# S5 power tables summed in one piece and written by ScalarE; the x2 sums on VectorE

## The chip, the cores and the metric

The kernel runs on one core of a Trainium2 chip. The metric is device time in microseconds (us), the median of several executions. One more execution was taken with the hardware profiler; all rows below are of that one.

Engine names as in the profile: PE is TensorE (matmuls), PEld its weight loads, DVE is VectorE, ACT is ScalarE, POOL is GpSimd, SP is SyncE, which here only issues DMAs.

## The reference, cut to what matters

One transformer block on a sequence of 1024 rows of width 1024, in fp32: four mixers side by side (dilated attention, retention, gated linear attention, an S5 state space layer), an output projection and a norm; a cross attention to a memory of 256 rows and a norm; a SwiGLU feed-forward layer (inner width 2816) and a norm.

The two places that the change touches are the S5 layer and the way into the feed-forward layer.

```python
bu_re = jnp.einsum('bsgi,gpi->bsgp', ug, bb_re)
bu_im = jnp.einsum('bsgi,gpi->bsgp', ug, bb_im)
...
_, _, x_re, x_im = lax.associative_scan(combine, (at_re, at_im, bu_re, bu_im), axis=1)
y = (jnp.einsum('bsgp,gip->bsgi', x_re, c_re) - jnp.einsum('bsgp,gip->bsgi', x_im, c_im)
     + d * ug)
...
return (jax.nn.silu(x @ w_gate) * (x @ w_up)) @ w_down
```

S5 has 16 groups with 64 complex states and 16 channels each. The kernel takes the sequence in steps of eight, so it needs the powers 1 to 8 of each state's complex decay, times the input matrix (tables W) and times the output matrix (tables C).

## The kernel before, in words

**Order of the work.** The program is written as one Python class. `weave` interleaves, on PE, the steps of a mixer with matmul groups of the input projections (`fill_v`, `fill_fm`), so that PE has work while a mixer's small steps run on the other engines. The order in which each engine issues its instructions is then made by a planner with its own costs and simulated times; on the chip each engine works through its queue strictly in that order. fp32 matmuls are done as three products: `split` makes a rounded part on ScalarE (`whi`, `xv`: line 149) and the rest on VectorE (`wlo`, `xv`: line 150) from each operand.

**Buffers.** Tiles of 128 x 1024 come from one pool of 37 buffers through `big` (line 136), which begins each with a tiny GpSimd memset; these memsets are chained in program order, so a buffer that comes free late holds up all later ones. PSUM tiles of one tag have two buffers. Weights are loaded through three `wraw` buffers by SP's queue.

**S5 tables.** `s5_start` calls `s5_powers` four times: W for both halves h of the groups (products on VectorE), then C for both halves (products on GpSimd). Each call makes two tables (i = 0 and 1), each 128 partitions x 1024 columns. Partitions 0 to 63 hold one group of a pair (g = 0) and 64 to 127 the other (g = 1); the table has 32 columns for each power and each pair, 16 for g = 0 and 16 for g = 1, and where partition and column belong to different groups it is zero. Lines 1464 and 1465 form two products of 128 x 512 in a scratch tile `pab`; line 1468 zeroes with GpSimd the two quarters that must be zero, 64 x 512 each; lines 1473 to 1477 add or subtract the products with VectorE straight into the other two quarters, 64 x 512 each. That is two memsets and two sums for each of eight tables, 16 and 16 in all.

`s5_tables` (per half) transposes W on PE (`sV`), copies the result to SBUF with `copy`, which takes ScalarE and VectorE in turn (lines 185 and 186, two copies of 128 x 512 for each of four tables), multiplies W by a constant table on PE (`sK`), copies that (`sKt`, line 1502) on VectorE, and transposes it (`sKp`). `s5_rot` makes sines and cosines on VectorE and ScalarE. `s5_delays` loads shifted copies of the input (`s5D`) by DMA from `sur` in DRAM.

While this goes on, PE runs the projection `dv`: groups of 24 matmuls, its weights in three pieces. The third piece is 128 x 544, and its VectorE rest (`wlo`) is a VectorE instruction in the midst of the S5 tables.

**The turn to gate/up.** The feed-forward layer uses Strassen-like sums of blocks. `x2_turn` transposes the layer's input into four blocks `xr` (two tiles of 128 x 1024 each); `x2_sums` makes in place the differences T1 (`b12 - b11`), T2 (`b22 - T1`), T3 (`b22 - b12`) and T4 (`b21 - T2`), all by line 529, T1 and T2 on VectorE and T3 and T4 on GpSimd, and `x2_version` splits each into its two parts `xv` (ScalarE, then VectorE). `gu_first` runs for the first three of the column pairs while this goes on: matmuls with B11 into `gc`, copied to `ge` by ScalarE (line 681), then with B21 on top of it, then `h` (lines 686, 688). `gu_rest` uses the T products. GpSimd also makes sums of weight blocks (`sub`, line 631).

Of the kernel before, what the change touches and what calls it, by code (L numbers as in the profile page):

```python
# [15 lines left out]
ALU = mybir.AluOpType  # L16
PSUM = bass.MemoryType.PSUM

P = 128
# [18 lines left out]
class Kernel:  # L38
# [488 lines left out]

    def x2_sums(self):
        tt = lambda e, o, a, b, op: [e.tensor_tensor(out=o[i], in0=a[i], in1=b[i], op=op) for i in range(2)]
        v, g = self.nc.vector, self.nc.gpsimd  # L530
        b11, b12, b21, b22 = [self.xr[q] for q in ((0, 0), (0, 1), (1, 0), (1, 1))]
        tt(v, b11, b12, b11, ALU.subtract)
        self.x2_version("T1", b11)
        tt(v, b11, b22, b11, ALU.subtract)
        self.x2_version("T2", b11)
        self.qu = [self.big(n) for n in ("gq", "gu2")]
        tt(g, b12, b22, b12, ALU.subtract)
        self.x2_version("B22", b22)
        tt(g, b21, b21, b11, ALU.subtract)
        self.x2_version("T3", b12)  # L540
        self.x2_version("T4", b21)
        self.xr = None
# [911 lines left out]
    def s5_powers(self, src, t0, j0, neg, s, eng):  # L1454
        nc, v = self.nc, self.nc.vector
        pr, pi = [self.s5[q][:, j0:j0 + 4, t0:t0 + 8].unsqueeze(3).to_broadcast([P, 4, 8, 16]) for q in ("pr", "pi")]
        xr, xi = [src[i][:, j0:j0 + 4, :].unsqueeze(2).to_broadcast([P, 4, 8, 16]) for i in range(2)]
        out = []
        for i in range(2):
            w = s[i]  # L1460
            ab = self.big("pab")
            a, b = ab[:, :512], ab[:, 512:]
            a4, b4 = [q.rearrange("p (j t i) -> p j t i", j=4, t=8) for q in (a, b)]
            eng.tensor_tensor(out=a4, in0=pr, in1=(xr, xi)[i], op=ALU.mult)
            eng.tensor_tensor(out=b4, in0=pi, in1=(xi, xr)[i], op=ALU.mult)
            w4 = w.rearrange("p (j t i) -> p j t i", j=4, t=8)
            for g in range(2):
                nc.gpsimd.memset(w4[64 * g:64 * g + 64, :, :, 16 - 16 * g:32 - 16 * g], 0.0)
            for g in range(2):
                r = slice(64 * g, 64 * g + 64)  # L1470
                o = w4[r, :, :, 16 * g:16 * g + 16]
                if i == 0:
                    v.tensor_tensor(out=o, in0=a4[r], in1=b4[r], op=ALU.subtract)
                elif neg:
                    v.scalar_tensor_tensor(out=o, in0=a4[r], scalar=-1.0, in1=b4[r], op0=ALU.mult, op1=ALU.subtract)
                else:
                    v.tensor_tensor(out=o, in0=a4[r], in1=b4[r], op=ALU.add)
            out.append(w)
        return out

    def s5_tables(self, h):
        v = self.nc.vector
        j0 = 4 * h
        W, Cp = self.s5w[h]
        Vw = []
        kt = self.tr("sK").rearrange("p a b -> p (a b)")[:, :256]
        for i in range(2):
            o = self.big("s5V")
            t = self.two("sV")
            for b in range(2):  # L1490
                for q in range(4):
                    c = (4 * b + q) * P
                    self.tp(t[:, c:c + P], W[i][:, c:c + P])
            for b in range(2):
                self.copy(o[:, b * 512:(b + 1) * 512], t[:, b * 512:(b + 1) * 512])
            Vw.append(o)
            for jj in range(4):
                self.mm(kt[32 * jj:32 * jj + 32], self.s5["c0"][i][:, j0 + jj, :], W[i][:, jj * 256:jj * 256 + 256],
                        start=i == 0, stop=i == 1, tile_position=(0, 32 * jj))
            yield 0.88  # L1500
        ks = self.half("sKt")
        v.tensor_copy(ks[:, :256], kt)
        yield 1.7
        kp = self.tr("sKp")
        for dd in range(2):
            self.tp(kp[:, dd, :], ks[:, dd * P:(dd + 1) * P])
        K = self.s5k[h]
        v.tensor_copy(K, kp[:, :2, :].rearrange("p a b -> p (a b)"))
        self.s5t.append((Vw, K.rearrange("p (b a c) -> p a b c", a=4, b=2), Cp))
# [110 lines left out]

    def s5_start(self):
        nc = self.nc
        W = [self.s5_powers(self.s5["bb"], 0, 4 * h, False, [self.big("s5W") for _ in range(2)], nc.vector)
             for h in range(2)]
        C = [self.s5_powers(self.s5["c"], 8, 4 * h, True, [self.big("s5C") for _ in range(2)], nc.gpsimd)
             for h in range(2)]
        self.s5w, self.s5t = list(zip(W, C)), []
        self.s5r = self.s5_rot(0)
        self.s5D = [self.big("s5D") for _ in range(4)]
        self.s5d3 = [d.rearrange("p (s c) -> p s c", c=P) for d in self.s5D]  # L1630
# [195 lines left out]
```

## Time and profile before

| what | value |
|---|---|
| time, median of 3 runs | 1474.85 us (1470.94 to 1479.25) |
| the profiled execution's own time | 1470.48 us |
| its span, first to last instruction | 1468.7 us |
| PE busy | 1428.1 us (97%) |
| DVE busy | 938.7 us (64%) |
| ACT busy | 522.0 us (36%) |
| POOL busy | 340.8 us (23%) |

The busy share of an engine is an average over stages that are limited by different things. What decides a stage is which engine the others wait for there. The time outside the span (1470.48 against 1468.7) is 1.8 us.

### The profile page before, as it was taken

To read this page: it belongs to the slowest core of one execution; us is meant where nothing else is said; L and a number is where in the kernel's file an instruction comes from. 1 tells how busy PE (TensorE), PEld (TensorE's weight loads), DVE (VectorE), ACT (ScalarE), POOL (GpSimd) and SP (SyncE) were. 2 spreads that over 40 slices of the span, in tenths; PEclk is the share of its full clock that TensorE was granted. 3 is DMA by queue.
4 is the path that set the end of the run, shared out by engine and by line. 5 is a ranking of instruction groups with operands and counts; after the bars stand their busy time and mean duration, and the time that the engine had idled before them with its cause. 6 is when DMAs were issued, how large, how long until landed. Compare 5 with 4: busy or idle time off the path is not lost.

```text
span 1468.7 us, 20723 instructions
## 1 busy us (share of the span) xinstructions
PE 1428.1 (97%) x7778; PEld 1167.7 (80%) x7778; DVE 938.7 (64%) x1622; ACT 522.0 (36%) x828; POOL 340.8 (23%) x598
## 2 busy tenths in 40 slices
PE   8699999999999999999999989999999999999997
PEld 6587778778788888888888768888888888888885
DVE  7978545475467479548557986576655556554557
ACT  4124433352244124334344532222222224434324
POOL 6300000010000000000000466776666640000003
PEclk9899999999999999999999999999999999999999
DMA  6442111010338302214312425544444447666612
GB/s 225 143 104 94 34 58 44 15 58 2 127 110 301 101 30 72 74 56 137 121 36 95 158 79 186 185 168 165 165 166 166 163 166 278 219 194 191 195 41 108
DMA packets 71508, 184.70 MB, mean 126 GB/s; under 512 B 8544, under 2 KB 9328, under 8 KB 71408
## 3 DMA queue, kind: packets, MB, share of 16 engines
q1 hardware_dynamic: 69680, 180.23, 37.1%
q10 hardware_dynamic: 1728, 3.15, 0.6%
q8 instruction: 61, 1.00, 0.3%
q14 instruction: 39, 0.32, 0.1%
HBM read 141.79 MB, written 41.55 MB: 125 GB/s over the span
## 4 chain that ended last, share of the span: by engine, by line
PE 85%; DVE 8%; DMA 3%; issue 2%; ACT 1%; POOL 1%; SPq 0%; DVEq 0%; POOLq 0%; ACTq 0%
PE ga L73 11%; PE fm L73 8%; PE gb L73 7%; PE gc L73 7%; PE da L73 7%; PE q L73 6%; PE wo L73 6%; PE mx L73 5%; PE dr L73 5%; PE dn L73 3%; PE ds L73 2%; PE gv L73 2%; PE s L73 2%; DVE wlo L150 2%; PE pv L73 1%
## 5 line engine op out<-in xcount | busy, mean ns | idle before, releaser
L150 DVE TENSOR_TENSOR wlo<-wraw,whi 128x1024 fp32r<-128x1024 f32 (+3 forms) x177 | 230.2, 1303 | 126.1 <-ACT whi L149 125.2
L149 ACT CAST whi<-wraw 128x1024 fp32r<-128x1024 f32 (+3 forms) x177 | 183.2, 1038 | 289.5 <-PE da L73 56.5
L73 PE MATMUL ga<-xv,whi 128*128 128x512 f32 x528 | 163.1, 390 | 3.8 <-DVE gq L696 3.8
L73 PEld LDWEIGHTS ga<-xv,whi 128*128 128x128 f32 x528 | 98.7, 188 | 26.1 <-issue 5.8
L73 PE MATMUL gc<-xv,whi 128*128 128x512 f32 x352 | 110.7, 396 | 5.1 <-ACT ge L681 5.0
L73 PE MATMUL gb<-xv,whi 128*128 128x512 f32 x352 | 108.4, 389 | 0.0
L73 PE MATMUL ga<-xv,wlo 128*128 128x512 f32 x264 | 102.8, 389 | 0.0
L73 PE MATMUL fm<-xh,whi 128*128 128x512 f32 x208 | 86.0, 414 | 0.0
L73 PEld LDWEIGHTS gc<-xv,whi 128*128 128x128 f32 x352 | 66.7, 191 | 20.0 <-ACT ge L681 6.0
L73 PE MATMUL wo<-whi,oT 128*128 128x512 f32 x256 | 82.1, 394 | 0.0
L73 PE MATMUL fm<-xh,wlo 128*128 128x512 f32 x208 | 81.5, 392 | 0.0
L73 PE MATMUL fm<-xl,whi 128*128 128x512 f32 x208 | 81.3, 391 | 0.0
L73 PE MATMUL mx<-whi,yT 128*128 128x512 f32 x256 | 80.6, 392 | 0.1
L73 PEld LDWEIGHTS gb<-xv,whi 128*128 128x128 f32 x352 | 66.1, 188 | 13.8
L73 PE MATMUL gc<-xv,wlo 128*128 128x512 f32 x176 | 69.2, 393 | 0.0
L73 PE MATMUL gb<-xv,wlo 128*128 128x512 f32 x176 | 68.5, 389 | 0.0
L263 POOL TENSOR_TENSOR X<-X,ln_ff_b 128x1024 f32<-128x1024 f32 x7 | 16.7, 2387 | 209.6 <-ACT X L262 209.6
L73 PEld LDWEIGHTS ga<-xv,wlo 128*128 128x128 f32 x264 | 49.6, 188 | 10.3
L73 PEld LDWEIGHTS mx<-whi,yT 128*128 128x128 f32 x256 | 48.1, 188 | 10.8 <-DVE V L150 0.5
L73 PE MATMUL da<-whi 128*128 128x512 f32 x144 | 56.2, 390 | 0.0
L73 PE MATMUL da<-whi,wlo 128*128 128x512 f32 x144 | 56.0, 389 | 0.0
L73 PE MATMUL da<-wlo,whi 128*128 128x512 f32 x144 | 56.0, 389 | 0.0
(500 smaller groups left out, 3332.3 us busy)
## 6 DMA issues: line engine op xcount, KB each, us to landing
wraw<-in_w_gu SPq DMA_DIRECT2D x28, 512.0 KB, 4.1
gr<-in_w_gu SPq DMA_DIRECT2D x22, 512.0 KB, 4.9
dw<-in_w_down SPq DMA_DIRECT2D x18, 512.0 KB, 3.7
tT<-dw SPq DMA_DIRECT2D x36, 256.0 KB, 2.0
wraw<-hS SPq DMA_DIRECT2D x36, 256.0 KB, 2.7
wraw<-tT SPq DMA_DIRECT2D x36, 256.0 KB, 3.0
wraw<-in_w_q SPq DMA_DIRECT2D x16, 512.0 KB, 4.3
wraw<-in_w_o SPq DMA_DIRECT2D x16, 512.0 KB, 3.5
```

What stands on the lines that cost most here:

```text
L73: return self.pin(self.nc.tensor.matmul(*a, **k))
L149: return (self.nc.scalar.copy(out=hi, in_=src), self.nc.vector.tensor_tensor(out=lo, in0=src, in1=hi.bitcast(F32), op=ALU.subtract))
L150: self.nc.vector.tensor_tensor(out=lo, in0=src, in1=hi.bitcast(F32), op=ALU.subtract))
L263: nc.gpsimd.tensor_tensor(out=x, in0=x, in1=b, op=ALU.add)
```

## The change

In `s5_powers` the two products are now added or subtracted once, over all 128 partitions, in place in `pab`. ScalarE then writes the sum twice, into the columns of g = 0 and of g = 1, each time multiplied by a column of a small table `gmul` with one value for each partition: 1 (or -1, for the negated tables) on the partitions of that group and 0 on the others. So the zeros come out of the multiplication, and the 16 memsets are gone. `gmul` (128 x 4) is made once by eight memsets of 64 x 1. In `s5_tables` all copies of `sV` are put on ScalarE. In `x2_sums` the sums of T3 and T4 move from GpSimd to VectorE.

```diff
     def x2_sums(self):
...
-        v, g = self.nc.vector, self.nc.gpsimd
+        v = self.nc.vector
...
-        tt(g, b12, b22, b12, ALU.subtract)
+        tt(v, b12, b22, b12, ALU.subtract)
         self.x2_version("B22", b22)
-        tt(g, b21, b21, b11, ALU.subtract)
+        tt(v, b21, b21, b11, ALU.subtract)
...
             eng.tensor_tensor(out=b4, in0=pi, in1=(xi, xr)[i], op=ALU.mult)
-            w4 = w.rearrange("p (j t i) -> p j t i", j=4, t=8)
+            v.tensor_tensor(out=a, in0=a, in1=b, op=(ALU.subtract, ALU.add)[i])
+            w3, a3 = w.rearrange("p (q i) -> p q i", i=32), a.rearrange("p (q i) -> p q i", i=16)
             for g in range(2):
-                nc.gpsimd.memset(w4[64 * g:64 * g + 64, :, :, 16 - 16 * g:32 - 16 * g], 0.0)
-            for g in range(2):
-                r = slice(64 * g, 64 * g + 64)
-                o = w4[r, :, :, 16 * g:16 * g + 16]
-                if i == 0:
-                    v.tensor_tensor(out=o, in0=a4[r], in1=b4[r], op=ALU.subtract)
-                elif neg:
-                    v.scalar_tensor_tensor(out=o, in0=a4[r], scalar=-1.0, in1=b4[r], op0=ALU.mult, op1=ALU.subtract)
-                else:
-                    v.tensor_tensor(out=o, in0=a4[r], in1=b4[r], op=ALU.add)
+                m = 2 * (neg and i == 1) + g
+                nc.scalar.mul(out=w3[:, :, 16 * g:16 * g + 16], in_=a3, mul=self.gmul[:, m:m + 1])
             out.append(w)
...
             for b in range(2):
-                self.copy(o[:, b * 512:(b + 1) * 512], t[:, b * 512:(b + 1) * 512])
+                self.nc.scalar.copy(out=o[:, b * 512:(b + 1) * 512], in_=t[:, b * 512:(b + 1) * 512])
...
     def s5_start(self):
         nc = self.nc
+        self.gmul = self.small("gmul", [P, 4], bufs=1)
+        for m in range(4):
+            for g in range(2):
+                nc.gpsimd.memset(self.gmul[64 * g:64 * g + 64, m:m + 1], (1.0 - 2 * (m // 2)) if g == m % 2 else 0.0)
```

## Rows read from the trace of the kernel before

**Rows 1.** The page's part 1: busy us, share of the span, instructions.

```profile
PE 1428.1 (97%) x7778; PEld 1167.7 (80%) x7778; DVE 938.7 (64%) x1622; ACT 522.0 (36%) x828; POOL 340.8 (23%) x598
```

**Rows 2.** All waits of PE: waiter, releaser, total us, times, longest.

```profile
PE dv L73 <- DVE wlo L150: 5.9, 1, 5.9
PE gc L73 <- ACT ge L681: 5.0, 1, 5.0
PE ga L73 <- DVE gq L696: 3.8, 2, 3.3
PE sKp L76 <- DVE sKt L1502: 3.4, 1, 3.4
```

**Rows 3.** Three stretches: busy us of each engine, PEclk, DMA share, GB/s.

```profile
49.00:62.70 13.70, 7.81 (x55) 7.01 (x54) 13.48 (x16) 0.03 (x1) 7.15 (x16) 0.75 0.36 116
...
831.00:864.00 33.00, 27.97 (x115) 22.64 (x114) 32.79 (x25) 14.47 (x17) 14.16 (x16) 0.90 0.20 66
...
846.50:851.00 4.50, 4.48 (x11) 3.52 (x12) 4.50 (x3) 2.49 (x3) 3.41 (x4) 0.50 0.00 0
```

**Rows 4.** VectorE's queue in order of time, 44 to 73 us (start, length).

```profile
47.07 1.38 DVE L1473 TENSOR_TENSOR s5C<-pab 64x512 f32<-64x512 f32 x2
...
53.25 2.14 DVE L1475 SCALAR_TENSOR_TENSOR s5C<-pab 64x512 f32<-64x512 f32 x2
55.42 0.73 DVE L150 TENSOR_TENSOR wlo<-wraw,whi 128x544 fp32r<-128x544 f32 x1
56.06 2.24 DVE L1473 TENSOR_TENSOR s5W<-pab 64x512 f32<-64x512 f32 x2
...
64.00 1.39 DVE L1475 SCALAR_TENSOR_TENSOR s5C<-pab 64x512 f32<-64x512 f32 x2
...
68.96 0.68 DVE L186 COPY s5V<-sV 128x512 f32<-128x512 f32 x1
...
70.62 0.42 DVE L1502 COPY sKt<-sK 128x256 f32<-128x256 f32 x1
```

**Rows 5.** VectorE's groups by form, 44.4 to 73 us: busy us, mean ns.

```profile
L1367 DVE TENSOR_TENSOR s5ph<-s5ph,s5rot 128x512 f32<-128x512 f32 x1 | 0.7, 681 | 0.0
...
L1364 DVE TENSOR_SCALAR s5rot<-s5ph 128x512 f32<-128x512 f32 x1 | 0.4, 419 | 0.0
```

**Rows 6.** ScalarE by line (ns: least/median/most) and its longest idle time there.

```profile
L262 ACT ACTIVATE X<-X,lny x7: 1135/1148/1154, 1426.9 to 1460.2; 128x1024 f32<-128x1024 f32 x7
...
L185 ACT COPY s5V<-sV x4: 586/588/598, 64.2 to 75.7; 128x512 f32<-128x512 f32 x4
...
62.75 0.37 ACT L956 COPY dv<-dv 128x256 f32<-128x256 f32 x1 [13.72 <-POOL dv L136]
```

**Rows 7.** GpSimd's memsets by line 1468, those of W.

```profile
L1468 POOL MEMSET s5W<- x8: 518/520/520, 2.7 to 6.3; 64x512 f32 x8
```

**Rows 8.** VectorE's queue at the turn, 831 to 864 us.

```profile
833.20 7.90 DVE L150 TENSOR_TENSOR xv<-xr,xv 128x1024 fp32r<-128x1024 f32 x3
...
842.75 1.21 DVE L529 TENSOR_TENSOR xr<-xr,xr 128x1024 f32<-128x1024 f32 x1
...
845.02 3.37 DVE L529 TENSOR_TENSOR xr<-xr,xr 128x1024 f32<-128x1024 f32 x1
```

**Rows 9.** GpSimd's and ScalarE's queues at the turn.

```profile
832.28 6.59 POOL L529 TENSOR_TENSOR xr<-xr,xr 128x1024 f32<-128x1024 f32 x2 [1.12 <-DVE xr L529]
...
859.18 0.10 POOL L136 MEMSET gr<- 128x2 f32 x1 [1.03 <-DVE xv L150]
...
843.99 1.04 ACT L149 CAST xv<-xr 128x1024 fp32r<-128x1024 f32 x1 [5.94 <-DVE xr L529]
...
845.89 0.58 ACT L681 COPY ge<-gc 128x512 f32<-128x512 f32 x1
```

**Rows 10.** The chain that ended last, where the turn ends.

```profile
873.18 2.73 DVE wlo L150
...
876.65 5.69 PE ga L73 x24
```

## The prediction

> **What bounds the kernel now.** I read part 1 of the page first: PE is busy for 97% of the span [rows 1], so nothing counts that doesn't shorten or cause a wait of PE. The list of PE's waits comes next, and it is short: four waits make up most of it [rows 2], and all four lie in the two stages that the change touches. In the S5 stage PE's `dv` matmuls wait 5.9 us for a `wlo` of VectorE, and a transpose (`sKp`) waits 3.4 us for VectorE's copy `sKt`. At the turn to gate/up, `gc` waits 5.0 us for ScalarE's copy `ge`, and `ga` waits 3.3 us at a time for VectorE's `gq`.
>
> The windows then tell who is late there. From 49.0 to 62.7 us VectorE is busy 13.48 of 13.70 us and ScalarE 0.03; from 831 to 864 us VectorE is busy 32.79 of 33.00 [rows 3]. In both stages VectorE's queue is the limit, and ScalarE stands idle for 13.72 us in one piece in the first [rows 6]. The queues in order of time show what PE is waiting behind. The `wlo` of the third `dv` weight begins at 55.42, after four half-sums; `sKt` begins at 70.62, behind twelve more half-sums (56.06 to 65.4, of which the first and the last pair stand there) and a copy [rows 4].
>
> **S5, VectorE.** Sixteen sums of 64 x 512 go, eight of 128 x 512 come. An undisturbed pair of half-sums takes 1.39 us, two pairs took 2.14 and 2.24 [rows 4]; an addition of 128 x 512 with both operands in SBUF takes 0.68 [rows 5]. So half the partitions bring no shorter instruction, and eight instructions are simply saved. In front of the `wlo`: 1.38 + 2.14 = 3.52 becomes 2 x 0.68 = 1.36, a gain of 2.2. Between the `wlo` and `sKt`: 2.24 + 5 x 1.39 = 9.2 becomes 6 x 0.68 = 4.1, a gain of 5.1, and a copy of 0.68 moves to ScalarE. `sKt` would begin 2.2 + 5.1 + 0.7 = 8.0 earlier, at 62.6.
>
> PE's first wait shrinks by 2.2, to 3.7. PE reached the `sKp` transposes about 3.4 before 71.0 (70.62 + 0.42), at 67.6; now it comes 2.2 earlier, at 65.4, and `sKt` is done at 63.0. The second wait is gone, with 2.4 to spare. S5: 2.2 + 3.4 = 5.6 us. This keeps the planner's order. If it fills the first wait too, 5.9 is to be had there; if it puts the `wlo` behind other work, the gain becomes a loss (rival 3).
>
> **S5, ScalarE and GpSimd.** ScalarE gets sixteen writes of 128 x 512, with a scale for each partition. No row has that instruction. Nearest are the same scaled write over 1024 columns at 1.15 us and a plain copy of 128 x 512 at 0.59 [rows 6]: between 0.59 and, should it cost a whole 1024-column write, 1.15; I take 0.7, near the copy, since the length decides. With four more copies of 0.59 it is 16 x 0.7 + 4 x 0.59 = 13.6 us, at most 20.8. The idle piece before the first `dv` eviction is 13.72, so at 0.7 the writes just fit, and I cost them at nothing. If they don't fit, the eviction at 62.75 [rows 6] is late, and PE may run only two `dv` groups ahead (two PSUM buffers). GpSimd's sixteen memsets took 0.52 each, the last of W began at 6.3 us [rows 7], long before a sum needed them; their going, and the eight tiny memsets for `gmul`, I cost at nothing. A scratch buffer is now held until ScalarE's second write, some 1.4 us after the sum; the buffers behind it come later by that, but the sums themselves come 2 to 8 us earlier.
>
> The Trainium skill speaks against this part: "ScalarE: Activation LUTs", section "Rules for kernel authors", sends multiplication and addition to VectorE, as faster per element. The rows do show a one-operand VectorE instruction of 128 x 512 at 0.42 [rows 5] against ScalarE's 0.59. By the rule the sixteen writes would be VectorE's: 8 x 0.68 + 16 x 0.42 = 12.2 us there, against about 12.7 now, so S5 would gain next to nothing instead of 5.6. Here ScalarE is idle and VectorE is the late one, so I side with the rows.
>
> **The turn.** Four GpSimd sums leave, the first two at 832.28 taking 6.59 us [rows 9]. While they run, VectorE's instructions stretch. Three splits took 7.90 where one instruction of that size takes 1.21 alone, and a sum 3.37 [rows 8]; a `wlo` right after it is like that sum. Excess: 7.90 - 3 x 1.21 = 4.3, and twice 3.37 - 1.21 = 2.2, in all 8.6 us. Nothing else of GpSimd's that takes long stands between 832 and 859, so this excess should go whole. VectorE gets four sums of 1.21: 4.8. Net gain on its queue: 3.8.
>
> Which wait shows it: `ge`, issued at 845.89, stands on ScalarE's queue behind a cast that waited 5.94 for VectorE's T2 sum of 842.75 [rows 8, 9]. That sum follows the three splits, so `ge` comes 4.3 earlier, or 1.9 if two new sums (2.4) go ahead of it. But the end of the stage is set later: the memset of a weight buffer `gr` at 859.18 waits for VectorE's last splits [rows 9]; behind it come a load, GpSimd's weight sums, a `wlo` at 873.18, and PE again at 876.65 [rows 10]. This chain starts 3.8 earlier. PE, which got to that wait at 873.3 (876.65 - 3.3), gets there at 871.4 or sooner and goes on at 872.8. So the turn gives 3.8 in either order. Its bounds: nothing, if the planner puts other work in the freed places, and 5.0 + 3.3 plus half of the 4.5 us for which PE ran at a granted clock of 0.50 after its wait (1.2 of 2.4 GHz) [rows 3], 10.5.
>
> **Sum.** 5.6 + 3.8 = 9.4 us. The profiled execution took 1470.5, a span of 1468.7 and 1.8 around it: 1461.1. The median of the runs lies 4.4 above that execution, so the forecast for a median is 1474.85 - 9.4 = 1465.5. After either stage PE is full up to the end, so nothing should take the gain back.
>
> **The rivals.** All are counted from 1474.85.
>
> 1. The planner also closes what I leave: all four waits and the slow clock go, 5.9 + 3.4 + 10.5 = 19.8, giving 1455.0. For it: the re-planned queues have 8 us less on VectorE in S5. Against it: the planner had put the `wlo` at 55.42 though VectorE was there all the time, so its times are not the chip's.
>
> 2. ScalarE becomes the late engine in S5. At the upper price it has 20.8 us to do in 13.7, 7.1 too many; the slack of about 2.4 to `sKt` and the overlap of two PSUM groups go, and S5's 5.6 is given back. Only the turn is left: 1474.85 - 3.8 = 1471.0. For it: its queue is in order, and each write waits for a sum. Against it: the 1.15 is for twice the columns. This is also the direction in which the skill's rule on ScalarE points.
>
> 3. Slower: the third `dv` `wlo` falls behind all S5 work that VectorE has up to `sKt`. Without the hole in which it stood, the planner may let the sums and the rotation tables go first. That work ends at 62.6 by my sum, plus what stands beside `sKt`, 1 to 3 us: `wlo` near 65 instead of 55.4, and the first wait grows by 9.6. Against that the second wait and the turn give 3.4 + 3.8 = 7.2: 2.4 slower, 1477.3. It decides the sign once the `wlo` begins after 55.4 + 7.2 = 62.6. For it: S5's tables are written ahead of the `dv` loads. Against it: before, with more sums in the queue, it didn't come last.
>
> **How the numbers follow.** Forecast 0.45, rival 1 0.15, rival 2 0.25, rival 3 0.15. A difference of under 0.5% (7.4 us) can hardly be told from none here: the three runs alone spread over 8.3 us. The forecast's own range is 1461 to 1469. It ends in faster by over 0.5% for 0.40 of its 0.45; rival 1 adds 0.15; rival 2 all but 0.02 within; rival 3 is within for 0.09, beyond for 0.06. Faster 0.57, same 0.37, slower 0.06. The range goes from rival 1's 1455 to 1477, short of rival 3's time and beyond.
>
> **What would show it.** Right: sums of 128 x 512 near 0.68 on VectorE, eight of them; ScalarE busy from 49 to 63 us; the wait of `sKp` gone and that of `dv` below 4 us; at the turn no split or sum over 1.5 us between 831 and 855, and VectorE's last splits before 856. Wrong: scaled writes well above 0.8 us; `dv` waiting for ScalarE; the `wlo` after 60 us; or a new wait of PE anywhere else, as the whole order is planned anew.

## The result and the profile after

The changed kernel took 1491.33 us in the median of 4 runs (1491.2 to 1492.64), the kernel before 1474.76 (4 runs, 1470.94 to 1479.25). The ratio is 1.0111, with a 95% interval from 1.0092 to 1.0129: slower by about 16.6 us, where 9.4 us less had been forecast. The profiled execution took 1491.2, with a span of 1489.4 (before: 1470.5 and 1468.7).

Part 1 of the changed kernel's page answers to [rows 1]:

```profile
PE 1445.5 (97%) x7778; PEld 1165.6 (78%) x7778; DVE 921.6 (62%) x1614; ACT 533.6 (36%) x848; POOL 324.5 (22%) x586
```

VectorE and GpSimd have less to do and ScalarE a little more, as meant. But PE, with the same 7778 matmuls, is busy for 17.4 us longer. That is a thing apart from waits, and it is the larger half of the loss. The smaller half stands in the list of PE's waits (of all of PE's waits in the changed kernel, the first, the third and that of `gc`; they answer to [rows 2]):

```profile
PE dv L73 <- ACT gq L892: 18.3, 1, 18.3
...
PE ga L73 <- DVE gq L696: 2.2, 3, 1.5
...
PE gc L73 <- ACT ge L681: 1.0, 1, 1.0
```

Three of the four waits before are gone or small: `sKp` has none, `gc` has 1.0 for 5.0, and no wait of `ga` is above 1.5 (one was 3.3). But `dv` waits once for 18.3 us, for a ScalarE copy `gq` that stood in no row ahead of the prediction (it is of the first projection, line 892; the `gq` of line 696 is another tile, of gate/up).

**The new wait.** `gq` and `su` are the copies that empty the first projection's PSUM banks (lines 887 and 892). ScalarE's queue in order of time, in the kernel before, where they come as soon as PE is done:

```profile
44.68 1.08 ACT L887 COPY su<-p 128x512 f32<-128x512 f32 x2 [8.42 <-PE p L73]
46.04 1.08 ACT L887 COPY su<-p 128x512 f32<-128x512 f32 x2 [0.28 <-PE p L73]
47.00 0.60 ACT L892 COPY gq<-p 128x512 f32<-128x512 f32 x1
```

The same queue in the changed kernel:

```profile
47.19 1.33 ACT L1470 ACTIVATE s5C<-pab,gmul 128x512 f32<-128x512 f32 x2 [11.96 <-DVE pab L1466]
...
52.30 1.33 ACT L1470 ACTIVATE s5C<-pab,gmul 128x512 f32<-128x512 f32 x2 [3.24 <-DVE pab L1466]
53.70 4.03 ACT L1470 ACTIVATE s5W<-pab,gmul 128x512 f32<-128x512 f32 x6
57.64 1.05 ACT L887 COPY su<-p 128x512 f32<-128x512 f32 x2
58.58 1.34 ACT L1470 ACTIVATE s5W<-pab,gmul 128x512 f32<-128x512 f32 x2
59.81 1.32 ACT L1470 ACTIVATE s5C<-pab,gmul 128x512 f32<-128x512 f32 x2
61.04 1.06 ACT L887 COPY su<-p 128x512 f32<-128x512 f32 x2
61.98 1.35 ACT L1470 ACTIVATE s5C<-pab,gmul 128x512 f32<-128x512 f32 x2
63.22 0.58 ACT L892 COPY gq<-p 128x512 f32<-128x512 f32 x1
```

All sixteen scaled writes (2 + 2 + 6 + 2 + 2 + 2) stand ahead of the first `gq` copy, and the first of them holds the queue for 11.96 us, since its sum on VectorE is not done. The reader is to see an in-order queue: the copies need nothing that is late, but what stands ahead of them does. PE's queue and the window of its wait in the changed kernel (the columns of the window are as in [rows 3]):

```profile
63.85 0.60 PE L73 MATMUL dv<-whi,xh 128*128 128x272 f32 x1 [18.32 <-ACT gq L892]
```

```profile
47.19:65.20 18.01, 1.35 (x6) 1.35 (x7) 16.28 (x22) 14.58 (x25) 6.76 (x16) 0.51 0.31 108
```

The `dv` group begins 0.05 us after the first `gq` copy ends (63.22 + 0.58). PE ran no matmul in the 18.32 us ahead of 63.85, and the six of this window behind it; over the window its granted clock was 0.51, close to the lower of its two levels (1.2 of 2.4 GHz). The first matmul of the dilated attention (`do`), which follows the S5 stage, came at 162.5 us; before, at 153.3. The 9.2 between them is what the waits say: 18.3 came, 5.9 + 3.4 = 9.3 went. It is one execution of each kernel, and that of the kernel before was a fast one: in the traces of the experiments below, `do` comes at 153.0 (e9), 155.6 (e2) and 158.8 (e4) with the S5 order of before, at 162.1 (e8) and 163.0 (e5) with the changed one.

**The longer matmuls.** Matmuls of one tile by form (ns least/median/most, first to last start), kernel before, then the changed one:

```profile
L73 PE MATMUL mx<-whi,yT x256: 387/389/501, 480.6 to 572.9; 128*128 128x512 f32 x128
...
L73 PE MATMUL ga<-xv,whi x528: 387/389/467, 856.9 to 1242.4; 128*128 128x512 f32 x176
...
L73 PE MATMUL da<-whi x144: 389/389/459, 1267.3 to 1389.2; 128*128 128x512 f32 x144
```

```profile
L73 PE MATMUL mx<-whi,yT x256: 392/396/502, 490.3 to 585.0; 128*128 128x512 f32 x128
...
L73 PE MATMUL ga<-xv,whi x528: 389/396/502, 866.7 to 1263.0; 128*128 128x512 f32 x176
...
L73 PE MATMUL da<-whi x144: 389/389/458, 1288.0 to 1409.9; 128*128 128x512 f32 x144
```

The same matmuls take 396 ns in the median for 389, over whole stages; a matmul's time holds no wait. The ends of matmuls are modelled in these traces, so look at the starts too: in gate/up three matmuls began every 0.68 us before, and every 0.70 us in the changed kernel, 227 and 233 ns for one. This is the "spacing" of the expectations below:

```profile
1000.21 0.62 PE L73 MATMUL gb<-xv,whi 128*128 128x512 f32 x2
...
1000.89 0.62 PE L73 MATMUL gb<-xv,whi 128*128 128x512 f32 x2
```

```profile
1011.23 0.63 PE L73 MATMUL gb<-xv,whi 128*128 128x512 f32 x2
...
1011.93 0.63 PE L73 MATMUL gb<-xv,whi 128*128 128x512 f32 x2
```

From the first to the last `ga` it is 396.3 us for 385.5, from the first to the last `mx` 94.7 for 92.3. The `da` matmuls are not touched: 121.9 and 121.9. What tells them apart is where their operands lie: `mx` and `ga` take one from the weight buffers (`whi`) and one from the pool of 37 large buffers; `da` takes both from weight buffers. The other large groups of 512-column matmuls fall in line: `gb`, `q` and `wo`, with one operand from each, are slower as well (`gb` 396 ns in the mean for 389), `dr`, with both in weight buffers, and `dn`, with both in the pool, stay at 389. The change's own `gmul`, 16 bytes of each partition in a slot of 32, is allotted between the two and moves the weight buffers, which lie behind it, by 32 bytes, `whi` from 196224 to 196256; the pool begins at 16512 in both.

**The turn.** VectorE's queue there in the changed kernel answers to [rows 8]:

```profile
846.72 3.48 DVE L529 TENSOR_TENSOR xr<-xr,xr 128x1024 f32<-128x1024 f32 x3
850.13 2.34 DVE L150 TENSOR_TENSOR xv<-xr,xv 128x1024 fp32r<-128x1024 f32 x2
```

Three sums take 3.48 and two splits 2.34, where three splits had taken 7.90 and one sum 3.37. The first `ga` comes 41.5 us after the first `gc` (825.2 to 866.7); before, 48.0 (808.9 to 856.9).

Two theories follow, with a rival. **A**: the place of the weight buffers against the pool makes the matmuls longer, some 14 to 17 us. **B**: the copies that empty PSUM, queued behind the scaled writes, cost some 6 to 9 us, and the turn gives about 4 back. **The rival**: the longer matmuls come from the new order of work (other engines at the same memories, more busy DMA queues), so that a place alone does nothing.

### The profile page after: what moved, and what is told of

It is laid out like the page before. It is cut to its first block, busy times and chain, and to the rows that moved or that the text cites. A ratio compares the mean times of both kernels' runs of the same rounds, so it can differ in the third digit from the quotient of the medians.

```text
span 1489.4 us, 20734 instructions
## 1 busy us (share of the span) xinstructions
PE 1445.5 (97%) x7778; PEld 1165.6 (78%) x7778; DVE 921.6 (62%) x1614; ACT 533.6 (36%) x848; POOL 324.5 (22%) x586
## 4 chain that ended last, share of the span: by engine, by line
PE 85%; DVE 5%; DMA 3%; POOL 2%; issue 2%; ACT 2%; SPq 0%; DVEq 0%; POOLq 0%; ACTq 0%
PE ga L73 10%; PE fm L73 9%; PE gc L73 8%; PE gb L73 7%; PE da L73 7%; PE wo L73 6%; PE q L73 6%; PE mx L73 5%; PE dr L73 5%; PE dn L73 3%; PE ds L73 2%; PE dv L73 2%; PE gv L73 2%; PE s L73 2%; PE pv L73 1%
## 5 line engine op out<-in xcount | busy, mean ns | idle before, releaser
L150 DVE TENSOR_TENSOR wlo<-wraw,whi 128x1024 fp32r<-128x1024 f32 (+3 forms) x177 | 227.1, 1286 | 126.9 <-ACT whi L149 126.5
L73 PE MATMUL ga<-xv,whi 128*128 128x512 f32 x528 | 166.5, 396 | 2.3 <-DVE gq L696 2.2
L73 PEld LDWEIGHTS wo<-whi,oT 128*128 128x128 f32 x256 | 48.0, 188 | 11.1
```

The lines of the kernel that those rows point to most:

```text
L73: return self.pin(self.nc.tensor.matmul(*a, **k))
L150: self.nc.vector.tensor_tensor(out=lo, in0=src, in1=hi.bitcast(F32), op=ALU.subtract))
```

## The experiments

Each was timed beside runs of the kernel before on the same chip, whose medians were 1474.84 (e1 to e4), 1475.79 (e5 to e8) and 1475.32 (e9 to e11, on another chip, so that these are set beside the others by their ratios). Where an address counts, it is the one that the program allots, in bytes of a partition:

```
                          pool of 37   whi      whi against the pool, over before
before, e4                16512        196224     0
after, e1                 16512        196256   +32
e3                        16512        196288   +64
e6                        16512        196352  +128
e9                        16512        196480  +256
e2, e5, e7, e8, e10, e11  16544        196256     0
```

**e1: the kernel before, with an unused slot where `gmul` lies.** Every queue keeps its order; one tiny memset is added.

```diff
 self.nc.gpsimd.memset(z, 0.0)
+self.nc.gpsimd.memset(self.small("pad", [P, 4], bufs=1), 0.0)
```

> The kernel before with one unused tile of 128 x 4 more, put ahead of the weight buffers whi and wlo, and one small GpSimd memset of it. Every engine's queue keeps its order; the weight buffers begin 32 bytes later in each partition (196256 instead of 196224, so 32 past a multiple of 64), the pool of 37 buffers stays where it was. Theory A (the place of the weight buffers against the other operand sets the matmuls' spacing): 512-column products of the middle stages come 233 ns apart instead of 227, the matmuls of the last stage (both operands in the weight buffers) stay, and the time grows by about 18 us, to some 1492. Theory B (the wider spacing comes from what the other engines do at the time, so from the new order of the queues): nothing changes, 1474 within 4 us.

1491.62 us (1491.05 to 1492.14, 4 runs), ratio 1.0116 [1.01, 1.0133]: 16.8 us slower, from 32 bytes that nothing reads. The kernel's `ga` and `da` matmuls by form:

```profile
L74 PE MATMUL ga<-xv,whi x528: 392/396/498, 868.6 to 1263.9; 128*128 128x512 f32 x176
...
L74 PE MATMUL da<-whi x144: 387/389/458, 1288.9 to 1410.8; 128*128 128x512 f32 x144
```

It has the 396 ns of the changed kernel with none of its order, so the rival falls: the place alone does it. Nor does another engine have to be at work: of the starts of `ga`, `gb`, `gc`, `q`, `mx` and `wo` matmuls in this trace, the 107 beside which no VectorE, ScalarE or GpSimd instruction and no DMA packet runs stand 233.5 ns apart in the mean, the rest of them 233.3; in the kernel before 103 such stand 226.7 apart.

**e2: the kernel before, pool and weight buffers both moved by 32 bytes.** It parts "the weight buffers' own address" from "their distance to the pool".

```diff
+self.c0 = ctx.enter_context(tc.tile_pool(name="c0", bufs=1))
+self.nc.gpsimd.memset(self.c0.tile([P, 8], F32, tag="shift", name="shift"), 0.0)
 self.c4 = ...
```

> The kernel before with one unused tile of 32 bytes a partition ahead of everything, so that the pool of 37 buffers and the weight buffers both begin 32 past a multiple of 64, with the same distance as before. Theory A in its form on distance (only the place of one operand against the other counts): no change, 1474 within 4 us. Theory A in its absolute form (an operand that begins off a multiple of 64 is read more slowly): all 512-column matmuls slow down, those of the last stage too, 18 us or more, above 1490. Theory B: no change.

1474.68 us (10 runs), ratio 1.0003 [0.9991, 1.0016]: no change. Its `whi` lies where that of e1 lies, at 196256, and its matmuls are those of before:

```profile
L75 PE MATMUL ga<-xv,whi x528: 387/389/632, 860.2 to 1246.6; 128*128 128x512 f32 x176
```

So not the address but the distance between the two operands counts.

**e3: the changed kernel with the slot of e1 as well**, which moves `whi` by 64 bytes. The edit is that of e1.

> The changed kernel with the same unused tile of 128 x 4, so that with the table gmul the weight buffers lie 64 bytes further than before, at a multiple of 64 again; orders of all queues as in the changed kernel. Theory A: the spacing returns to 227 ns and about 18 us come back: 1473. Theory B: 1491, no change.

1489.75 us (4 runs, 1488.4 to 1491.63), ratio 1.0104 [1.0086, 1.0123]. The matmuls stay long (`ga` median 394 ns): 64 bytes are no better than 32.

**e4: the turn alone**, on the kernel before. No `gmul`, and PE's order is kept.

```diff
-tt(g, b12, b22, b12, ALU.subtract)
+tt(v, b12, b22, b12, ALU.subtract)
...
-tt(g, b21, b21, b11, ALU.subtract)
+tt(v, b21, b21, b11, ALU.subtract)
```

> The kernel before with the sums of T3 and T4 on VectorE alone; no new table, so no operand moves. By the trace of the changed kernel, in which the first matmul into ga came 6.5 us earlier against the stage before it: 6 us faster than before, 1468, with the waits of 5.0 and 3.3 us at the turn gone. By the prediction's sum: 3.8 us. If the turn's gain is paid back later: no change.

1471.3 us (10 runs, 1468.49 to 1475.26), ratio 0.9979 [0.9965, 0.9994]: 3.5 faster. Of its waits of PE, the first two and that of `gc`:

```profile
PE dv L73 <- DVE wlo L150: 7.1, 1, 7.1
PE ga L73 <- DVE gq L696: 3.5, 5, 1.7
...
PE gc L73 <- ACT ge L681: 1.3, 1, 1.3
```

The large waits of the turn are gone, but `ga` has five small ones left, 3.5 in all, as it catches up with VectorE. In S5, which this kernel doesn't change, `dv` waits 7.1: the 5.9 of [rows 2] was on the low side, since all five traces with that order of S5 (e1, e2, e4, e6, e9) show 7.0 to 7.3 there.

**e5: the changed kernel with `gmul` allotted ahead of the pool**, so that pool and weight buffers move together. The order stays.

```diff
+self.c0 = ctx.enter_context(tc.tile_pool(name="c0", bufs=1))
 self.c4 = ...
...
-self.gmul = self.small("gmul", [P, 4], bufs=1)
+self.gmul = self.c0.tile([P, 4], F32, tag="gmul", name=self.nm("gmul"))
```

> The changed kernel, with the table gmul laid ahead of the pool of 37 buffers instead of behind it: both the pool and the weight buffers begin 32 bytes later, so their distance is that of the kernel before, and all queues keep the order of the changed kernel. Theory A (only the distance counts): 512-column products come 227 ns apart again and about 17 us come back, to 1474; PE still waits 18 us for gq. Theory A* (what counts is that the weight buffers lie on a certain multiple, whatever the distance): stays at 1490.

1478.04 us (10 runs, 1474.75 to 1480.28), ratio 1.0015 [1.0003, 1.0027]. The place gives back 1491.33 - 1478.04 = 13.3 us, where about 17 were expected; `ga` is at 389 ns again. What is left against the kernel before, 2.2 us, is theory B less the gain of the turn. Its first row of waits and its `ga` matmuls:

```profile
PE dv L74 <- ACT gq L893: 18.4, 1, 18.4
```

```profile
L74 PE MATMUL ga<-xv,whi x528: 387/389/504, 859.2 to 1246.6; 128*128 128x512 f32 x176
```

**e6: e1 with 128 bytes** (`[P, 32]` for `[P, 4]`).

> The kernel before with an unused tile of 128 bytes a partition ahead of the weight buffers, orders unchanged. The distance between the two pools was a multiple of 512 bytes; 32 and 64 more made the matmuls slow. If 128 bytes is the step that counts, the spacing stays at 227 ns and the time at 1474; if it is 256 or 512, the products come 231 to 233 ns apart and the time is 1485 to 1492.

1488.68 us (2 runs, 1486.66 and 1490.69), ratio 1.0084 [1.005, 1.0117]: slow too, perhaps a little less. The median `ga` is 392 ns, but from the first to the last `ga` it is 395.5 us, as in e1 (395.3), so the lower median is no faster stage:

```profile
L74 PE MATMUL ga<-xv,whi x528: 387/392/628, 867.0 to 1262.5; 128*128 128x512 f32 x176
```

**e7: e5, and every scaled write ordered behind the six copies that empty PSUM.** In `proj_first` the four `su` copies and the two `gq` copies are kept in a list `self.ev`.

```diff
-nc.scalar.mul(out=w3[:, :, 16 * g:16 * g + 16], in_=a3, mul=self.gmul[:, m:m + 1])
+o = nc.scalar.mul(out=w3[:, :, 16 * g:16 * g + 16], in_=a3, mul=self.gmul[:, m:m + 1])
+for e in self.ev:
+    self.order(o, e)
```

> As e5, and ScalarE's scaled writes are ordered behind the six copies that empty the first projection's PSUM banks (su and gq); no other step changes, though the planner sets the queues anew. Theory C (PE's 18 us wait for gq comes only from the writes' place ahead of those copies): the wait goes below 1 us, the S5 stage ends 9 us earlier than in e5 or better, and the time is 1465 or less. Rival (the writes are too much for ScalarE wherever they stand, as the prediction's rival 2 had it): the wait moves to another place of the S5 stage and the time stays within 4 us of e5.

1464.91 us (4 runs, 1461.92 to 1467.32), ratio 0.9922 [0.9898, 0.9946]: 10.9 faster than before, 13.1 faster than e5. It beats both kernels. Its first waits of PE, and ScalarE's queue:

```profile
PE dv L74 <- DVE wlo L151: 4.9, 1, 4.9
PE ga L74 <- DVE gq L697: 4.0, 4, 1.8
```

```profile
47.18 0.61 ACT L893 COPY gq<-p 128x512 f32<-128x512 f32 x1
52.49 1.33 ACT L1472 ACTIVATE s5W<-pab,gmul 128x512 f32<-128x512 f32 x2 [4.70 <-DVE pab L1468]
```

The copies are back at 43.4 to 47.8 us, the writes follow, the wait for `gq` is gone, and so is that of `sKp`. `dv` waits for the `wlo` again, as the prediction had it. The planner moved little else. By the traces GpSimd has the order of e5; on ScalarE, besides the writes and the copies, a `whi` cast, a pair of `dv` copies and a pair of rotation steps have changed places, on VectorE a sum, a `wlo` and an `sKt`, all in the S5 stage. That sum now stands behind the `wlo` of the third `dv` weight and not ahead of it, so a part of the 13.1 us may be its. VectorE's queue just ahead of the `wlo`:

```profile
50.25 2.14 DVE L1468 TENSOR_TENSOR pab<-pab 128x512 f32<-128x512 f32 x2
52.32 1.57 DVE L151 TENSOR_TENSOR wlo<-wraw,whi 128x544 fp32r<-128x544 f32 x1
```

**e8: e5 with the turn undone** (the sums of `b12` and `b21` back on GpSimd), so S5's change alone, at the right place but in the planner's order.

> As e5, with the sums of T3 and T4 back on GpSimd: the S5 part alone, operands at the distance of before. If the S5 part costs what the traces show up to the first dilated products (9.2 us): 1484. If the x2 part gives nothing in the end: the time of e5.

1481.99 us (8 runs, 1479.79 to 1482.86), ratio 1.0037 [1.0024, 1.0051]: 6.2 slower, two thirds of the 9.2 that the two traces had shown. `dv` waits 18.4 for `gq`, as in e5, and the turn's waits are back:

```profile
PE gc L74 <- ACT ge L682: 5.4, 2, 5.3
PE ga L74 <- DVE gq L697: 3.9, 1, 3.9
```

Beside e5 it gives the turn once more: 1481.99 - 1478.04 = 4.0 us.

**e9: e1 with 256 bytes** (`[P, 64]`).

> The kernel before with an unused tile of 256 bytes a partition ahead of the weight buffers, orders unchanged. 32, 64 and 128 bytes more all made the products slow. If 256 is the step, the 512-column products come 227 ns apart (389 to 392 ns each in the groups) and the time is 1475; if only 512 or more is, they take 394 to 397 ns and the time is 1485 or more.

1474.52 us (8 runs, 1471.27 to 1476.64), ratio 0.9994 [0.9978, 1.001]: no change, with one unused buffer and one memset more than before, as in e1 and e6.

```profile
L74 PE MATMUL ga<-xv,whi x528: 389/389/628, 857.0 to 1243.2; 128*128 128x512 f32 x176
```

The matmuls are at 389 ns again. Moves of 0 and 256 bytes are free; 32 and 128 cost 16.8 and 12.9 us (e1, e6), and 64 about what 32 does (e3 is 1.6 faster than the changed kernel).

**e10: e7 with the sixteen scaled writes on VectorE**, as the rule of the Trainium skill would have it that the prediction weighed ("ScalarE: Activation LUTs", section "Rules for kernel authors").

```diff
-o = nc.scalar.mul(out=w3[...], in_=a3, mul=self.gmul[:, m:m + 1])
-for e in self.ev:
-    self.order(o, e)
+v.tensor_scalar(out=w3[...], in0=a3, scalar1=self.gmul[:, m:m + 1], scalar2=None, op0=ALU.mult)
```

> As e7, with the sixteen scaled writes on VectorE instead of ScalarE. By the rule on multiplications in the Trainium skill (ScalarE: Activation LUTs, Rules for kernel authors) VectorE is the place for them: no slower than e7, 1465. By the prediction's count (16 x 0.42 = 6.7 us more on the engine that is late): 5 to 7 us slower than e7, 1471, with the wait of dv for wlo longer than 5 us or the wait of sKp back.

1467.91 us (5 runs, 1465.95 to 1469.08), ratio 0.9945 [0.9925, 0.9966]: 3 us slower than e7 by the medians, 3.4 by the ratios, but the intervals overlap. On VectorE a write takes about 0.42:

```profile
61.62 1.67 DVE L1472 TENSOR_SCALAR s5W<-pab,gmul 128x512 f32<-128x512 f32 x4
```

Of the first waits of PE in it, the first and the third, which is new:

```profile
PE dv L74 <- DVE wlo L151: 3.4, 1, 3.4
...
PE sV L77 <- issue: 2.8, 1, 2.8
```

The rule's premise holds for these writes: VectorE is faster, 0.42 against 0.715. By the prediction's count `dv` should then wait longer, with 16 x 0.42 us more on VectorE; it waits less, 3.4 for 4.9, since the planner put the `wlo` ahead of most of the writes (at 50.66; in e7 at 52.32). Which engine should have the writes isn't settled by these runs.

**e11: e7 with the third `dv` weight asked for ahead of S5's tables**, and VectorE's products and sums ordered behind its `wlo`, to fill the wait that e7 leaves.

```diff
+self.items_all()
+while len(self.wi) < 3:
+    self.wi.append(self.loadw(*self.wq.pop(0)))
 self.s5_start()
-self.items_all()
...
+for q in p:   # the products on VectorE, and the sum
+    self.order(q, self.last_load[2])
```

> As e7, with the third dv weight loaded earlier in the program and VectorE's table products and sums ordered behind its wlo. The whi cast was done at 38 us in e7 and the wlo began at 52.3, so nothing but its place in the queue held it. If so, the wait of dv (4.9 us) goes to nothing and the time falls by 4 to 5 us against e7, to 1460; if the tables, now later by one wlo, become the late ones, the wait of sKp comes back and the gain is under 2 us.

1466.26 us (5 runs, 1465.02 to 1467.6), ratio 0.9931 [0.9909, 0.9953]: no gain over e7. The `wlo` now stands at 45.30 and nobody waits for it. The first of PE's waits:

```profile
PE dv L74 <- ACT glow L959: 4.1, 1, 4.1
```

and the end of the scaled writes on ScalarE's queue, with what stands behind them:

```profile
60.61 1.34 ACT L1474 ACTIVATE s5C<-pab,gmul 128x512 f32<-128x512 f32 x2 [0.45 <-DVE pab L1468]
61.85 0.35 ACT L958 COPY dv<-dv 128x256 f32<-128x256 f32 x1
62.10 0.17 ACT L959 COPY glow<-dv 128x16 f32<-128x16 f32 x1
```

The `dv` copies come as soon as the writes end, at 61.85, and PE waits for them. In e7 the same wait for `glow` is 0.9 us. ScalarE is the next late engine; the 4.9 us that e7 leaves weren't had by moving the `wlo` alone.

## Why the prediction was wrong

**What the loss is made of.** The place: 1.0111 in the changed kernel against 1.0015 in e5 is 0.0096 x 1475 = 14.2 us (e1, alone, 16.8). S5 in the planner's order: 6.2 (e8). The turn: -4.0 (e8 against e5). Together 14.2 + 6.2 - 4.0 = 16.4, measured 16.6. The two agree because the three are differences along one chain of runs (changed kernel, e5, e8, before); that the parts have these sizes is borne out by e1 for the place and by e4 (-3.5) for the turn. Mended at both places, the change takes 1464.91 (e7), where the forecast was 1465.5. That this is so near is partly luck, since the parts of it are not those of the forecast, as said below.

**The step that failed first: eight tiny memsets for `gmul`, "I cost at nothing".** Their time is nothing. What they write is a new buffer, for which 32 bytes of each partition are allotted, and the prediction never asked where it lies. Shown: that its place makes the matmuls longer (e1), that the distance between weight buffers and pool decides and not the address (e2 against e1, at one and the same address of `whi`), that 32, 64 and 128 bytes cost and 256 doesn't (e1, e3, e6, e9). Nothing in the trace of before could show it; the allocations would have shown the shift, but not its price.

**The step that failed second: ScalarE's sixteen writes costed at nothing, because they "just fit" in the idle piece from 49.03 to 62.75.** The size was right: 0.7 us for one, 0.715 measured. The groups by form, 30 to 70 us, of the changed kernel:

```profile
L1470 ACT ACTIVATE s5C<-pab,gmul 128x512 f32<-128x512 f32 x8 | 5.3, 717 | 15.2 <-DVE pab L1466 15.2
L1470 ACT ACTIVATE s5W<-pab,gmul 128x512 f32<-128x512 f32 x8 | 5.2, 715 | 0.2
...
L1466 DVE TENSOR_TENSOR pab<-pab 128x512 f32<-128x512 f32 x8 | 7.6, 1000 | 0.0
```

The third column has it: the writes held ScalarE's queue for 15.2 us while it waited for VectorE's sums. The prediction looked at who reads the writes (`sKt`, the `dv` copies behind the idle piece) and not at what ScalarE had to do just ahead of the idle piece: six copies, at 44.68 to 49.03, on which PE's next banks hang. The new order put them behind. "`dv` waiting for ScalarE" stood among the signs of a wrong prediction, but rival 2 had it as a matter of throughput, at which S5's 5.6 are given back and no more; as a matter of order S5 ends 6.2 slower than before (e8). Rival 3 had the right kind of mistake, a job planned behind S5 work, for the wrong job and engine: the `wlo` stood at 55.05, as before. Shown by e7 against e5, where the order of the six copies and the writes is the edit and the other orders are those of e5 up to a few instructions of the S5 stage: 13.1 us, and the wait gone. The writes' number, rival 2, is the smaller matter: behind the copies they cost PE a wait of 0.9 us in e7, and of 4.1 in e11, where the wait for the `wlo` no longer hides them.

**VectorE in S5: right in kind, one size off.** The eight sums do replace sixteen half-sums, but at a mean of 1.00 us and not 0.68: an undisturbed one takes 0.68, and those that run beside GpSimd's products for the `s5C` tables are stretched, as the half-sums were [rows 4]. In e7 `dv` waits 4.9 where 3.7 was forecast, the wait of `sKp` is gone as forecast. Against the 7.1 that is usual with the order of before, 4.9 is the forecast's gain of 2.2, but by other terms: three sums and not two stand ahead of the `wlo` and take 0.69 + 2.14 = 2.83 where 1.36 was forecast, the `wlo` takes 1.57 for 0.73, and VectorE's products ahead of them take 0.68 or 0.69 each, where two of them had been stretched to 1.86 and 1.53. That it comes out at this size is luck. S5 gives 10.9 - 3.5 = 7.4 in e7 against e4, 5.6 forecast; the two were timed on different occasions, and the intervals allow for either.

**The turn: right in size and in its cause.** 3.8 forecast, 3.5 (e4) and 4.0 (e8 against e5) measured. No split or sum is stretched any longer: the groups by form of VectorE in the changed kernel, 846 to 876 us:

```profile
L150 DVE TENSOR_TENSOR xv<-xr,xv 128x1024 fp32r<-128x1024 f32 x10 | 11.9, 1209 | 0.0
L529 DVE TENSOR_TENSOR xr<-xr,xr 128x1024 f32<-128x1024 f32 x8 | 9.4, 1209 | 0.0
```

The Trainium skill ("SBUF — State Buffer", section "SBUF: two separate sides") states that VectorE instructions with two SBUF inputs and GpSimd instructions that read SBUF exclude each other for a whole instruction; the 1209 ns here, against 7.90 us for three [rows 8], agree. The way there was the forecast's in the main. From the first `gc` to the first `ga` it is 41.5 us for 48.0 (e4: 40.6): the wait of `gc` goes whole, and the granted clock over this stretch is 1.00 in e4 for 0.93 before, both of which the forecast had as its upper bound. Some 3 of it are paid back: from the first to the last `ga`, e4 takes 388.7 us for 385.5, with waits of PE of 6.0 us in all for 3.8. The memset of `gr` with which the forecast's chain begins comes 46.8 us after the first `gc` (e4: 47.0) where it was 50.3: 3.5 and 3.3 earlier, with 3.8 forecast. One sign did not come: VectorE's last splits end 49.0 us after the first `gc`, before 51.4, where 'before 856' asks for 47.1.

**"After either stage PE is full up to the end, so nothing should take the gain back": false.** PE is full there (its longest waits in gate/up are 1.5 us), and its matmuls got longer. The sentence took the length of a matmul for a constant of the kernel.

**What stays open.** What in the chip links the distance of two operands to the pace of matmuls; only distances of 0, 32, 64, 128 and 256 bytes more than before were tried. Not every matmul with one operand from each side is slower: those of 256 columns (`rv<-wlo,xh`) take 280 ns in the changed kernel and 279 in e1 for 282 before. Whether the writes are better on VectorE (e10) isn't settled at 3 us with overlapping intervals.

## What to carry to other kernels

When work goes to an idle engine, read what stands on its queue just ahead of the idle time and who waits for that: an instruction that waits for a late engine is harmless only behind the copies that empty PSUM for PE, and an order that the planner is free to change has to be tied down. When a change allots even a few bytes, look at what it shifts, and put small new buffers where the large ones keep their distance. If PE's busy time grows with the same count of matmuls, compare the median of one matmul form, and the distance of its starts, ahead of any theory on waits.

## What the runs showed of the hardware

The pace of f32 matmuls of 512 columns (128x128 weights) depends in this kernel on where their two operands lie against each other in SBUF. With the weight buffers 32 bytes further from the pool, the median goes from 389 to 396 ns, the stretch of `ga` matmuls from 385.5 to 395.3 us (e1), the kernel by 16.8 us of 1475. With 64 bytes it is 394 ns, with 128 it is 392 and 12.9 us (of two runs); with 256 nothing, and nothing when both move by 32. Matmuls with both operands in weight buffers (`da`) stay at 389 throughout, and the longer pace is there with the other engines and the DMA queues idle (e1). That the distance counts modulo 256 bytes would fit all five; it is argued from these, not shown.
